# Last layer, left half: the residual add on GpSimd instead of VectorE, its stores issued by ScalarE

## The chip, the cores and the metric

One core of a Trainium2 chip runs the whole program in one launch. The metric is device microseconds. Before the change three runs took 2939.29 us in the median (2937.05 to 2940.01). The engines are called as in the profile: PE is TensorE (PEld its weight loads), DVE is VectorE, ACT is ScalarE, POOL is GpSimd, SP is SyncE. Each engine works through its own instructions strictly in the order in which they were written; engines wait for one another by semaphores.

## The reference

Two layers work on 1024 latent tokens and 256 context tokens of 1024 channels: first a convolution module, then grouped-query attention, each followed by a SwiGLU. The last layer (i = 1) is, cut to what the change touches:

```
yx, yc = attention_module(hx, hc, ...)                       # ends in @ wo
x  = x + g_x * rmsnorm(yx, norm_g[1, 1])                     # residual: the add that is moved
fx = rmsnorm(x, norm_g[1, 2]) * (1.0 + scf_x) + shf_x        # input of the FFN
x  = x + gf_x * rmsnorm((silu(fx @ w1) * (fx @ w3)) @ w2, norm_g[1, 3])
```

All of it is float32. Layer 1 no longer carries the context tokens.

## The kernel before, in words

Activations lie transposed: channels on the 128 partitions in 8 tiles (k = 0 to 7, `KT`), tokens along the free dimension. The latent tokens go in two halves of 512, left and right. To get float32 exactness from TensorE each operand is split in a high and a low part (`hi`, `lo`), and each product is three matmuls: hi·hi, hi·lo, lo·hi (L172 to L174 in `mm3`, L183 to L185 in `mm3s`). ACT writes the high part, DVE the low one.

In the last layer attention runs as a stream of units (scores L1116, softmax L1122 and L1124, transposes L1134, their split into `T2` by ACT at L1137 and DVE at L1138, and the products with V at L1140 and L1141). The left half's attention comes first. While it ends, the right half's attention is put in as background work: `pump` takes a few steps of it after each step of the foreground. So the left half's output projection, its two norms and its FFN are written into the same instruction streams as the right half's attention.

Between the left half's output projection and its FFN stands `post_pre2` (L738). PE sums squares into columns (L746). DVE works out two reciprocal roots by Newton steps on 128x4 numbers (L343 to L351): `r1` for the norm of the attention output, `r2` for the norm of the new x. PE spreads each over the partitions (L735). For each k the loop then does

- L761: y = y * column * p1, on DVE, with p1 a copy of the first spread in SBUF (`sm`);
- L763: y = y + xr, the residual add (xr is the tile `HS` in the left half);
- L764: the store of y to `x3d` in HBM, read again for the last residual some 600 us later;
- `apply`: t = y * column * p2 on DVE (L399, p2 still in PSUM), hi = t + shift on ACT (L404, into `T6`), lo = t + shift - hi on DVE (L405, into `T3`).

The FFN's first step (ft = 0) multiplies w1 and w3 with these hi and lo, k by k: six matmuls of 128x512 for each k at L183 to L185, 48 in all, called the first sweep here. Its next step begins at L172, with w1 of ft = 1.

`post_pre2` is called twice: for the left half (L1521, `keep` False) straight through, without background steps between, and for the right half (L1529, `keep` True) as background work. A scheduler in the framework below orders what each engine issues by priority, so the written order of a loop isn't kept; the orders below are those of the built programs.

Of the kernel before, what the change touches and what calls it, by code (L numbers as in the profile page):

```python
# [12 lines left out]
ALU = mybir.AluOpType  # L13
# [42 lines left out]
class Kern:  # L56
# [681 lines left out]
    def post_pre2(self, ybox, xv, ps, xdst, ftags, box, keep=False):  # L738

        nc = self.nc  # L740
        (y, yacc), more, xr = ybox
        accs = (yacc, *more)
        for i, acc in enumerate(accs):
            for j in range(4):
                with self.later():
                    nc.tensor.matmul(ps[:, 4 * i + j:4 * i + j + 1], lhsT=acc[:, j * P:(j + 1) * P],  # L746
                                     rhs=self.c["ones"], start=True, stop=True)
        ys = [ps[:, 4 * i:4 * i + 4] for i in range(3)]
        v = self.tiny([P, 16], "nv")[:, :4]
        nc.vector.tensor_scalar(out=v, in0=ys[0], scalar1=1.0 / D, scalar2=EPS, op0=ALU.mult, op1=ALU.add)  # L750
        r1 = self.rsqrt(v, 4)
        p1 = self.sm(512)
        nc.scalar.copy(p1, self.spread(r1, self.bank("st")))
        r2 = self.rsqrt(self.add_sq(ys, r1, xv), 4)
        p2 = self.spread(r2, self.bank("st"))
        yield self.pace
        hi, lo = self.halves(*ftags, 512)
        box.append((hi, lo))
        for k in range(KT):
            yk = y[:, k, :]  # L760
            nc.vector.scalar_tensor_tensor(out=yk, in0=yk, scalar=self.col[1][0][1][:, k:k + 1], in1=p1,  # L761
                                           op0=ALU.mult, op1=ALU.mult)
            nc.vector.tensor_tensor(yk, yk, xr[:, k, :], op=ALU.add)  # L763
            nc.gpsimd.dma_start(xdst[:, k], yk)  # L764
            self.apply(yk, p2, 1, 2, ((0, 512, 0),), hi, lo, k, xr[:, k, :] if keep else None)
            yield 2 * self.pace

# [956 lines left out]
```

## Time and profile before

| what | value |
|---|---|
| median of three runs | 2939.29 us |
| profiled execution, its own time | 2938.98 us |
| its span, first to last instruction | 2937.2 us |
| around the span | 1.8 us |
| PE, DVE, ACT, POOL busy | 97%, 74%, 45%, 8% |
| mean granted TensorE clock | 0.987 of full speed |

A busy share is an average over stages that have different limits: PE is busy for nearly the whole span, so what counts is where it stands still. Times in the rows are from the start of the span, and a record may overlap the next one of its engine: where instructions follow each other without a wait, the time between two starts is what one costs.

### The profile page before, as it was taken

The numbers are of one execution on the slowest core, as the hardware profiler recorded it, in microseconds if no ns is written. First come the engines' busy times: TensorE is split into PE (matmuls) and PEld (weight loads), VectorE is DVE, ScalarE is ACT, GpSimd is POOL, SyncE is SP. The second block draws the span as 40 slices with busy tenths as digits, with TensorE's granted clock in tenths as the row PEclk, the third lists the DMA queues.
The fourth block names the chain that finished last, engine by engine and source line by source line (L and its number), as shares of the span: only waits on it lengthen the run. The fifth ranks groups of instructions, "written<-read, shape, count | busy, mean of one in ns | idle before, by whom it ended". The sixth has DMA issues, their size and how long they took to land.

```text
span 2937.2 us, 42731 instructions
## 1 busy us (share of the span) xinstructions
PE 2847.7 (97%) x16462; PEld 2446.1 (83%) x16462; DVE 2160.7 (74%) x3746; ACT 1335.5 (45%) x2229; POOL 222.6 (8%) x377
## 2 busy tenths in 40 slices
PE   7999989999999999999999999989999999999998
PEld 6888877888888889989888787767777778889997
DVE  6887788847556378877786899786666666786777
ACT  5222255532222245544445688645555543444444
POOL 0000001011022001000011111110000000010000
PEclk9999999999999999999999999999999999999999
DMA  6443444334356224333345211322222143353332
GB/s 249 140 120 98 116 131 145 135 116 143 115 175 198 65 74 165 114 104 112 109 156 170 88 46 46 97 87 81 66 73 83 60 149 99 110 170 104 102 98 75
DMA packets 131755, 336.58 MB, mean 115 GB/s; under 512 B 31328, under 2 KB 52864, under 8 KB 130656
## 3 DMA queue, kind: packets, MB, share of 16 engines
q1 hardware_dynamic: 78016, 222.33, 24.1%
q0 software_dynamic: 29344, 103.83, 10.7%
q10 hardware_dynamic: 24192, 7.70, 1.1%
q8 instruction: 129, 2.11, 0.3%
q14 instruction: 74, 0.61, 0.1%
HBM read 289.50 MB, written 38.93 MB: 112 GB/s over the span
## 4 chain that ended last, share of the span: by engine, by line
PE 86%; DVE 7%; ACT 2%; issue 2%; DMA 2%; ACTq 0%; POOL 0%; SPq 0%; DVEq 0%; POOLq 0%
PE ps L172 15%; PE ps L173 15%; PE ps L174 15%; PE ps L875 4%; PE ps L877 4%; PE ps L876 4%; PE ps L1116 4%; PE ps L1134 4%; PE ps L1140 2%; PE ps L454 2%; PE ps L455 2%; PE ps L456 2%; PE ps L1141 2%; PE ps L185 1%; PE ps L183 1%
## 5 line engine op out<-in xcount | busy, mean ns | idle before, releaser
L172 PE MATMUL ps<-T,wh 128*128 128x512 f32 (+1 forms) x1360 | 502.5, 370 | 1.4 <-ACT T L161 0.8
L174 PE MATMUL ps<-T,wl 128*128 128x512 f32 (+1 forms) x1360 | 500.4, 368 | 2.0 <-DVE wl L148 2.0
L173 PE MATMUL ps<-T,wh 128*128 128x512 f32 (+1 forms) x1312 | 481.4, 367 | 0.2 <-DVE T L164 0.2
L144 ACT CAST wh<-wr 128x1024 fp32r<-128x1024 f32 (+1 forms) x217 | 225.0, 1037 | 419.9 <-PE ps L173 307.2
L148 DVE TENSOR_TENSOR wl<-wr,wh 128x1024 fp32r<-128x1024 f32 (+1 forms) x217 | 261.9, 1207 | 168.5 <-ACT wh L144 167.1
L875 PE MATMUL ps<-T,wh 128*128 128x256 f32 x1092 | 310.7, 285 | 5.0 <-ACT wh L161 4.5
L876 PE MATMUL ps<-T,wh 128*128 128x256 f32 x1092 | 306.5, 281 | 0.0
L877 PE MATMUL ps<-T,wl 128*128 128x256 f32 x1092 | 305.4, 281 | 0.2 <-DVE wl L164 0.2
L1138 DVE TENSOR_TENSOR T<-ps,T 128x512 fp32r<-128x512 f32 x320 | 216.8, 687 | 107.6 <-ACT T L1137 106.8
L172 PEld LDWEIGHTS ps<-T,wh 128*128 128x128 f32 x1360 | 257.8, 190 | 43.7 <-ACT T L1506 1.7
L174 PEld LDWEIGHTS ps<-T,wl 128*128 128x128 f32 x1360 | 257.7, 190 | 42.4 <-DVE wl L148 2.2
L173 PEld LDWEIGHTS ps<-T,wh 128*128 128x128 f32 x1312 | 248.5, 189 | 38.2 <-DVE T L164 1.3
L1137 ACT CAST T<-ps 128x512 fp32r<-128x512 f32 x320 | 186.0, 586 | 191.1 <-PE ps L1134 177.6
L173 PE MATMUL ps<-HS,wh 128*128 128x512 f32 x656 | 257.9, 393 | 0.0
L172 PE MATMUL ps<-HS,wh 128*128 128x512 f32 x608 | 238.4, 392 | 0.9 <-ACT wh L144 0.9
L174 PE MATMUL ps<-HS,wl 128*128 128x512 f32 x608 | 237.5, 391 | 0.0
L875 PEld LDWEIGHTS ps<-T,wh 128*128 128x128 f32 x1092 | 206.1, 189 | 11.2 <-ACT wh L161 6.7
L876 PEld LDWEIGHTS ps<-T,wh 128*128 128x128 f32 x1092 | 206.6, 189 | 0.5
L877 PEld LDWEIGHTS ps<-T,wl 128*128 128x128 f32 x1092 | 206.2, 189 | 0.6 <-DVE wl L164 0.4
L1134 PE MATMUL ps<-cst,T 128*128 128x128 f32 x1100 | 189.6, 275 | 3.2 <-DVE T L1138 3.1
L1122 DVE TENSOR_SCALAR_CACHE_REDUCE T<-ps,rq 128x1280 f32<-128x1280 f32 x110 | 170.0, 1546 | 27.9 <-PE ps L1116 22.1
L1134 PEld LDWEIGHTS ps<-cst,T 128*128 128x128 f32 x1100 | 132.6, 141 | 49.5 <-DVE T L1138 30.8
(377 smaller groups left out, 6195.9 us busy)
## 6 DMA issues: line engine op xcount, KB each, us to landing
wr<-in_w SPq DMA_DIRECT2D x170, 512.0 KB, 3.6
wr<-in_pw SPq DMA_DIRECT2D x35, 512.0 KB, 3.5
HV<-in_wmodT POOLq DMA_DIRECT2D x56, 256.0 KB, 4.1
q<-in_wmodT POOLq DMA_DIRECT2D x56, 256.0 KB, 3.9
KB<-in_w SPq DMA_DIRECT2D x24, 512.0 KB, 3.6
HR<-in_w SPq DMA_DIRECT2D x23, 512.0 KB, 3.7
q<-in_w SPq DMA_DIRECT2D x23, 512.0 KB, 4.2
q<-qsd POOLq DMA_DIRECT2D x32, 256.0 KB, 3.3
```

What stands on the lines that cost most here:

```text
L144: nc.scalar.copy(hi, raw)
L148: nc.vector.tensor_tensor(lo, raw, hi.bitcast(F32), op=ALU.subtract)
L172: nc.tensor.matmul(out[:, :n], lhsT=wh, rhs=xh, start=k == 0, stop=False)
L173: nc.tensor.matmul(out[:, :n], lhsT=wh, rhs=xl, start=False, stop=False)
L174: nc.tensor.matmul(out[:, :n], lhsT=wl, rhs=xh, start=False, stop=k == nk - 1)
L875: nc.tensor.matmul(out, lhsT=wh, rhs=bh, start=first and k == 0, stop=False, **skip)
L876: nc.tensor.matmul(out, lhsT=wh, rhs=bl, start=False, stop=False, **skip)
L877: nc.tensor.matmul(out, lhsT=wl, rhs=bh, start=False, stop=k == 3, **skip)
L1122: nc.vector.tensor_scalar(out=pt, in0=sc, scalar1=rq[:, h:h + 1], scalar2=None, op0=ALU.mult, op1=ALU.min, accum_out=mn)
L1134: nc.tensor.transpose(tp[:, h * P:(h + 1) * P], Ps[h][:, j * P:(j + 1) * P], c["ident"])
L1137: nc.scalar.copy(ph, tp)
L1138: nc.vector.tensor_tensor(pl, tp, ph.bitcast(F32), op=ALU.subtract)
```

## The change

In the left half the add L763 goes from DVE to POOL, and the eight stores L764 from POOL's queue to ACT's. The right half (`keep` True) stays as it was.

```
             nc.vector.scalar_tensor_tensor(out=yk, in0=yk, scalar=self.col[1][0][1][:, k:k + 1], in1=p1,
                                            op0=ALU.mult, op1=ALU.mult)
-            nc.vector.tensor_tensor(yk, yk, xr[:, k, :], op=ALU.add)
-            nc.gpsimd.dma_start(xdst[:, k], yk)
+            (nc.vector if keep else nc.gpsimd).tensor_tensor(yk, yk, xr[:, k, :], op=ALU.add)
+            (nc.gpsimd if keep else nc.scalar).dma_start(xdst[:, k], yk)
             self.apply(yk, p2, 1, 2, ((0, 512, 0),), hi, lo, k, xr[:, k, :] if keep else None)
```

The scheduler answers with another order on four engines; SP's is unchanged. In the pieces below `T_16045` is y, `HS` is xr, `sm` is p1, `sb` is t, `T_16582` and `T_16583` are hi and lo; `T_13569` and `T_14068` are softmax rows of the right half's attention and `T_13571` their transposed split; `nr`, `nq` and `nh` are the 128x4 numbers of the Newton steps.

First place: POOL ahead of the FFN, the difference (lines with + are the change's).

```order
 L1147 COPY sb<-sums 128x256
 L1450 DMA od<-sb 128x2x128
-L764 DMA x3d<-T_16045 128x512 x8
+L763 ISA
+L763 TENSOR_TENSOR T_16045<-T_16045,HS 128x512 x8
 L1147 COPY sb<-sums 128x256
 L1102 DMA q<-qsd 128x4x128
```

The eight stores are gone from POOL; in their place stand the eight adds, and ahead of them one instruction without operands that the builder puts in (it has the engine load the code that the adds need, and waits for nothing).

The same place on DVE, the end of its piece of the difference: the last steps of the loop's first part and of the Newton steps for r2.

```order
-L763 TENSOR_TENSOR T_16045<-T_16045,HS 128x512 x2
+L351 SCALAR_TENSOR_TENSOR nr<-nq,nr 128x4
+L761 SCALAR_TENSOR_TENSOR T_16045<-T_16045,col_7910,sm 128x512
+L349 TENSOR_TENSOR nq<-nr 128x4
+L761 SCALAR_TENSOR_TENSOR T_16045<-T_16045,col_7910,sm 128x512
+L350 TENSOR_TENSOR nq<-nq,nh 128x4
+L1138 TENSOR_TENSOR T_13571<-ps,T_13571 128x512
+L351 SCALAR_TENSOR_TENSOR nr<-nq,nr 128x4
 L399 SCALAR_TENSOR_TENSOR sb<-T_16045,col_7912,ps 128x512 x3
```

DVE now runs all eight L761 in a row, each followed by one small Newton step, then one L1138 of the attention and the last Newton step; before, six L761 and six L763 stood there, and two of each followed further down.

Second place: ACT from the copy of p1 to the FFN's first weights, the whole difference.

```order
 L753 COPY sm<-ps 128x512
 L1137 CAST T_13571<-ps 128x512
+L764 DMA x3d<-T_16045 128x512 x8
+L1137 CAST T_13571<-ps 128x512
 L404 ACTIVATE T_16582<-sb,mod_103 128x512 x8
-L1137 CAST T_13571<-ps 128x512
 L144 CAST wh<-wr_73 128x1024
 L838 ACTIVATE sm<-ps 128x512
```

All eight stores, and a cast of the attention, now stand ahead of the first L404.

Third place: PE between the end of the left half's norms and the first sweep, one piece of the difference.

```order
 L1140 MATMUL ps<-T_13571,HR 128x512
+L1134 MATMUL ps<-cst,T_13569 128x128
 L735 MATMUL ps<-cst,nr 128x128 x4
+L1134 MATMUL ps<-cst,T_14068 128x128
+L1134 MATMUL ps<-cst,T_13569 128x128
+L1134 MATMUL ps<-cst,T_14068 128x128
+L1141 MATMUL ps<-T_13571,HR 128x512
+L1140 MATMUL ps<-T_13571,HR 128x512
 L183 MATMUL ps<-T_16582,wh 128x512 x2
```

Four transposes, one L1141 and one L1140 of the attention have moved ahead of the sweep; by L172 of ft = 1 both programs have issued the same matmuls, and from there on the orders are equal but for waits.

## Rows read from the trace of the kernel before

**Rows 1.** The page: the chain that ended last, shares by engine.

```profile
PE 86%; DVE 7%; ACT 2%; issue 2%; DMA 2%; ACTq 0%; POOL 0%; SPq 0%; DVEq 0%; POOLq 0%
```

**Rows 2.** Chain in order of time, 1941 to 1952: start, length, engine, line.

```profile
1941.33 0.75 DVE T L761
...
1948.45 1.20 DVE T L763 x2
1949.66 0.67 DVE sb L399
1950.35 0.73 ACT T L404
1951.12 1.22 PE ps L183 x2
```

**Rows 3.** Windows: stretch, length, busy of five engines, granted clock, DMA share, GB/s.

```profile
1945.00:1950.00 5.00, 1.11 (x4) 0.71 (x4) 5.00 (x12) 0.00 (x0) 1.68 (x5) 0.50 0.53 202
1950.00:1955.00 5.00, 3.87 (x9) 2.62 (x10) 5.00 (x9) 2.72 (x5) 0.49 (x1) 0.53 0.27 105
1955.00:1960.00 5.00, 5.00 (x23) 4.05 (x22) 5.00 (x8) 1.36 (x3) 0.20 (x1) 1.00 0.00 0
```

**Rows 4.** Timeline of DVE: start, length, line, operation, idle before.

```profile
1941.33 0.75 DVE L761 SCALAR_TENSOR_TENSOR T<-T,col,sm 128x512 f32<-128x512 f32 x1
...
1942.07 0.75 DVE L761 SCALAR_TENSOR_TENSOR T<-T,col,sm 128x512 f32<-128x512 f32 x1
```

**Rows 5.** Line L763: durations in ns (min, median, max), first and last start.

```profile
L763 DVE TENSOR_TENSOR T<-T,HS x8: 683/684/684, 1942.8 to 1959.4; 128x512 f32<-128x512 f32 x8
```

**Rows 6.** Timeline of POOL, 1895 to 1945.

```profile
1921.87 0.71 POOL L1450 DMA_DIRECT2D od<-sb  x1 [6.04 <-DVE sb L1156]
1943.79 1.22 POOL L764 DMA_DIRECT2D x3d<-T  x2 [21.21 <-DVE nr L351]
```

**Rows 7.** POOL's work on SBUF: its copies L1147, its small fills.

```profile
L1147 POOL COPY sb<-sums x32: 394/402/1365, 1605.4 to 2363.0; 128x256 f32<-128x256 f32 x32
...
L1271 POOL MEMSET KB<- 128x16 f32 x3 | 0.2, 113 | 48.8 <-PE ps L242 48.8
```

**Rows 8.** Timelines of DVE and POOL at the longest of these copies.

```profile
2133.81 1.22 DVE L148 TENSOR_TENSOR wl<-wr,wh 128x1024 fp32r<-128x1024 f32 x1
2134.95 0.68 DVE L1138 TENSOR_TENSOR T<-ps,T 128x512 fp32r<-128x512 f32 x1
...
2133.91 1.36 POOL L1147 COPY sb<-sums 128x256 f32<-128x256 f32 x1
```

**Rows 9.** Issues of DMAs from ACT's queue: durations in ns.

```profile
L472 ACTq DMA_DIRECT2D KB<-HR x64: 552/622/1559, 63.5 to 346.9; - x64
...
L1604 ACTq DMA_DIRECT2D outT<-T x1: 385/385/385, 2932.8 to 2932.8; - x1
```

**Rows 10.** Timeline of ACT, 1940 to 1967.

```profile
1950.35 2.04 ACT L404 ACTIVATE T<-sb,mod 128x512 fp32r<-128x512 f32 x3 [8.57 <-DVE sb L399]
...
1965.88 0.58 ACT L1137 CAST T<-ps 128x512 fp32r<-128x512 f32 x1
1966.35 1.06 ACT L144 CAST wh<-wr 128x1024 fp32r<-128x1024 f32 x1
```

**Rows 11.** Timeline of PE, 1941 to 1968.

```profile
1947.85 1.11 PE L735 MATMUL ps<-cst,nr 128*128 128x128 f32 x4 [5.51 <-DVE nr L351]
...
1962.16 0.60 PE L1134 MATMUL ps<-cst,T 128*128 128x128 f32 x4
1962.51 0.48 PE L1141 MATMUL ps<-T,HR 128*128 128x512 f32 x1
1962.83 0.41 PE L184 MATMUL ps<-T,wh 128*128 128x512 f32 x1
...
1967.40 0.50 PE L172 MATMUL ps<-T,wh 128*128 128x512 f32 x1 [0.39 <-DVE sm L839]
```

**Rows 12.** The page: DMA issues, with KB and median us to landing.

```profile
HV<-in_wmodT POOLq DMA_DIRECT2D x56, 256.0 KB, 4.1
```

## The prediction

> **What bounds the kernel now.** I read first the chain that ended last, by engine: 86% of it is PE and 7% DVE [rows 1]. So most stages are limited by matmuls, and work taken off DVE pays only where PE waits for DVE. The chain in order of time shows such a place at the change: from 1941.33 to 1950.35 us it runs over L761, L763 and L399 on DVE, then over one L404 on ACT, and at 1951.12 the first sweep starts on PE [rows 2]. The windows say the same in shares: from 1945 to 1950 DVE is busy 5.00 of 5.00 us, ACT 0.00 and PE 1.11, with a granted clock of 0.50, the lower of TensorE's two levels (1.2 GHz); it is 0.53 in the next 5 us and 1.00 from 1955 on, so PE pays for its rest a little beyond it [rows 3]. Here the add stands on the path that sets the end. From L172 at 1967.40 [rows 11] both orders are the same and PE goes on nearly without a gap, so I take the shift of that L172 as the change of the whole time.
>
> **What leaves DVE.** Ahead of the first L399 stood six L763. Each record is 684 ns [rows 5]; in the chain two of them take 1.20 us [rows 2], so 0.60 us each and 3.6 us in all. In their place come the two L761 that stood further down and one L1138 of the attention. Two L761 start 0.74 us apart with a small Newton step between them [rows 4], so all eight take 8 x 0.74 = 5.9 us, from 1941.33 to 1947.25; L1138 adds about 0.6 (its record is 0.68 [rows 8]), and the last Newton step ends at about 1948.0. Before, the spread L735 that waits for that step started at 1947.85 [rows 11]. So the reciprocal root is no earlier than it was: the order has eaten the gain. Undisturbed, L399 would start at about 1949.2 in place of 1949.6, a gain of 0.4 us and no more.
>
> **What POOL does in its place.** No add of two arrays on POOL is in this trace, so I bound it. Its copies of 128x256 take 402 ns in the median, its small fills 113 ns [rows 7]: about 0.1 us to start, and 0.30 for 256 elements. For 512 elements, with the second input read beside the first for nothing, that makes 0.1 + 0.6 = 0.7 us; with the two inputs read one after the other, 0.1 + 1.2 = 1.3 us. I take 1.1, above the middle, since only the upper end has a mechanism; eight adds are then 8.8 us. The Trainium skill ("GPSIMD Engine Reference", section Performance versus the Vector engine) has 4497 ns for such an add of 2048 elements; a quarter of that is 1.12, and by it the sum would be 0.2 us more. No run here shows it.
>
> **Can the adds run beside L761?** This decides the result. Of the 32 copies on POOL one took 1365 ns, against 402 in the median [rows 7]. It started at 2133.91, just after L148 on DVE had begun at 2133.81, and it ended at 2135.27, about 0.3 us after DVE had gone on to its next instruction at 2134.95 [rows 8]. L148 reads two arrays in SBUF (`wr` and `wh`); the L1138 that followed reads one and PSUM, and the copy finished beside it. I read this as: POOL's reading of SBUF stood still until DVE's two-input instruction was through. L761 reads y and p1, both in SBUF, and the small Newton steps behind each read two as well. So the 5.9 us of DVE work and the 8.8 us of adds go one after the other, in whatever turns: the last add ends at 1941.33 + 5.9 + 8.8 + 0.1 for a first wake-up = 1956.1. The Trainium skill states it as a rule ("SBUF — State Buffer", section Who interferes with whom): a DVE instruction with two SBUF inputs and a GpSimd instruction that reads SBUF exclude each other, and the one that comes second waits for the whole of the other. By that rule, the trace agrees in the one place that can show it; without it the last add would end at 1942.2 + 8.8 = 1951.0, which is the first rival's sum.
>
> **What stands behind the adds on ACT.** ACT stood idle for 8.57 us ahead of its first L404 at 1950.35 [rows 10], so eight issues have room there. But in the new order all eight stores are ahead of L404, each waits for its add, and ACT works in order: the first L404, which needs only the first add, now waits for the last. That is the wait the change adds. Behind it stand PE's sweep (it needs hi) and DVE's L405. Issues from ACT took 385 and 622 ns [rows 9]; I take 0.5 for the last, the others hide between adds. With 0.1 for the signal ACT is free at 1956.7. Then come the moved cast L1137, 0.47 from its start to the next one's [rows 10], and L404 with 0.73 [rows 2]: the sweep starts at about 1957.95, 6.8 us later than 1951.12. The two last stores also wait for two loads of SP's, lanes of the same counters; these were issued long before and have landed: nothing. POOL's eight issues go (two in 1.22 us [rows 6]); POOL was waiting between them, so that gains nothing. The store itself is read hundreds of us later.
>
> **What is given back.** Three transposes of a group of four, one L1141 and a gap have left the sweep, and run while PE waits: from 1962.16 to 1962.51 the four, to 1962.83 the L1141 [rows 11], so 0.26 + 0.32, and 0.16 of waiting near 1961.5. That is 0.7 us. PE restarts on the lower clock before and after, so this costs the same. DVE keeps ahead: its L405 come in threes at 0.66 us each, while PE needs six matmuls for each k.
>
> **Sum.** 6.8 - 0.7 = +6.1 us, if DVE gets its eight L761 and the last Newton step through early. If the turns alternate, that step stands behind the last add, and the spread (1.11 us [rows 11]) and some transposes come after it on the path: 1.3 us more, +7.4. I take the middle, +6.7. On the profiled execution's 2938.98 (span 2937.2 and 1.8 around it) that is 2945.7 us. The median of the runs, 2939.29, is 0.3 above that execution, which I leave out. With adds at 0.7 and at 1.3 us the sum goes to 6.1 - 3.2 = +2.9 and 7.4 + 1.6 = +9.0: the forecast's own range is 2941.9 to 2948.0.
>
> **The rivals.**
>
> First, no exclusion: the adds overlap L761, and the one long copy had another cause. The last add ends at 1951.0, ACT is free at 1951.6, the sweep starts at 1952.8, 1.7 late, less 0.7: +1.0 us, 2940.0. For it: it is one copy in 32. Against it: the length fits L148 to 0.3 us, and the typical copies that I could set beside DVE's work ran beside instructions with one SBUF input.
>
> Second, on the other side: no exclusion and quick adds. Below 0.98 us each, unhindered, the last store no longer holds L404 beyond what the transposes give back, and the change gains. At 0.7 the gate is L399 again: sweep at 1950.7, 0.4 early, and 0.7 given back: -1.1 us, 2937.9. It needs both the absent exclusion and the lower bound.
>
> Third, the instruction ahead of the adds. POOL has nothing to do from 1922.6 to the first add at 1942.1, 19.5 us [rows 6], so I cost it at nothing. If the code comes in only with the first add, POOL starts late. This trace has no such load; with about 4 us, as a DMA of 256 KB takes to land [rows 12], it would be +4 on top, 2949.7. The Trainium skill ("GPSIMD Engine Reference", section Architecture, Instruction dispatch) has about 6 us for the first call to freshly loaded code, which would make 2951.7; no run here shows it.
>
> **How the numbers follow.** Forecast 0.80, first rival 0.10, second 0.04, third 0.06. A measurement of this kernel can tell about 0.2%, 5.9 us, from no change. The forecast's sums lie on both sides of that bound, from +2.9 to +9.0 with the middle at +6.7; I give two thirds of it to slower, 0.54, and 0.26 to same. With the third rival slower is 0.60. Both first rivals are within the bound: same is 0.26 + 0.10 + 0.02 = 0.38, and 0.02 is left for faster. The range has to reach the first rival below (2940.0) and just past the forecast's upper end: 2940.0 to 2948.5.
>
> **What would show it.** In the changed profile: eight L763 on POOL, with about 14 us from the first L761 to the end of the last add; records or start distances on POOL or of L761 on DVE well above 1.1 and 0.74 us while both run, which would be the exclusion; the first L404 right behind the last store on ACT; PE's first L183 near 1958, and L172 of ft = 1 near 1974. If the adds start 0.74 us apart from 1942.2 and L761 keeps its pace, the exclusion is wrong. If the first L183 starts before L764's last issue, the wait on ACT is wrong. If L172 is late and the end isn't, the claim is wrong that PE carries the shift to the end.

## The result, and the profile after

| | median us | runs (lowest to highest) | ratio to before, 95% interval |
|---|---|---|---|
| before, all runs | 2940.90 | 15 (2937.05 to 2944.93) | |
| the change | 2945.76 | 15 (2940.74 to 2948.58) | 1.0017 [1.0010, 1.0024] |

The 15 runs of the kernel before take in the three that were known ahead; their median is 1.6 us higher than that of the three (2939.29). The change is slower by 4.9 us; the interval makes that 2.9 to 7.1 us. Its profiled execution has a span of 2944.6 us against 2937.2, 7.4 us more.

The windows of the changed kernel, with the columns of [rows 3], show PE standing still for nearly ten microseconds, 1945 to 1955, in which DVE and POOL are both busy:

```profile
1945.00:1950.00 5.00, 0.00 (x0) 0.00 (x0) 5.00 (x8) 0.00 (x0) 4.15 (x3) 0.50 0.40 157
1950.00:1955.00 5.00, 0.09 (x1) 0.09 (x1) 5.00 (x7) 0.00 (x0) 4.37 (x4) 0.50 0.27 105
1955.00:1960.00 5.00, 4.60 (x13) 3.03 (x14) 3.74 (x6) 2.43 (x4) 0.46 (x1) 0.50 0.27 105
1960.00:1965.00 5.00, 5.00 (x19) 3.94 (x19) 5.00 (x9) 2.04 (x3) 0.74 (x1) 0.82 0.00 0
```

PE (first column after the length) did 1.11 and 3.87 us of work in the first two stretches before; now 0.00 and 0.09. Both engines look busy, but a record that lasts long isn't work: the timelines of the two show it. First DVE (start, length, line, operation):

```profile
1940.76 0.75 DVE L761 SCALAR_TENSOR_TENSOR T<-T,col,sm 128x512 f32<-128x512 f32 x1
1941.43 0.16 DVE L349 TENSOR_TENSOR nq<-nr 128x4 f32<-128x4 f32 x1
1941.51 0.75 DVE L761 SCALAR_TENSOR_TENSOR T<-T,col,sm 128x512 f32<-128x512 f32 x1
1942.17 1.22 DVE L350 TENSOR_TENSOR nq<-nq,nh 128x4 f32<-128x4 f32 x1
1943.31 1.83 DVE L761 SCALAR_TENSOR_TENSOR T<-T,col,sm 128x512 f32<-128x512 f32 x1
1945.07 0.15 DVE L351 SCALAR_TENSOR_TENSOR nr<-nq,nr 128x4 f32<-128x4 f32 x1
1945.14 0.74 DVE L761 SCALAR_TENSOR_TENSOR T<-T,col,sm 128x512 f32<-128x512 f32 x1
...
1954.18 0.68 DVE L1138 TENSOR_TENSOR T<-ps,T 128x512 fp32r<-128x512 f32 x1
1954.78 0.70 DVE L351 SCALAR_TENSOR_TENSOR nr<-nq,nr 128x4 f32<-128x4 f32 x1
```

Then POOL, with the idle time before it in brackets:

```profile
1941.60 2.99 POOL L763 TENSOR_TENSOR T<-T,HS 128x512 f32<-128x512 f32 x2 [21.16 <-DVE nq L349]
1945.22 3.00 POOL L763 TENSOR_TENSOR T<-T,HS 128x512 f32<-128x512 f32 x2 [0.63 <-DVE nr L351]
1948.84 3.00 POOL L763 TENSOR_TENSOR T<-T,HS 128x512 f32<-128x512 f32 x2 [0.63 <-DVE nq L350]
1952.46 2.99 POOL L763 TENSOR_TENSOR T<-T,HS 128x512 f32<-128x512 f32 x2 [0.63 <-DVE nq L349]
```

A Newton step on 128x4 numbers, L350, that takes 0.16 us elsewhere took 1.22, and the L761 behind it 1.83 in place of 0.75; then the next pair of short records. There are four such turns, the last with L1138 and the final L351 in the place of an L761. One turn of two L761 and two adds lasts 1945.22 - 1941.60 = 3.62 us. Two L761 at a pace of 0.66 and two adds at 1.14 (from the start of the held L350 to the next start, 1943.31 less 1942.17) make 3.60. Since the 1.14 is read from the same turn, an add that nothing hinders is the better test: it takes 1.25 us (p1_in_psum below), and with it the sum is 3.82. So no more than 0.2 us of a turn overlaps. From the first L761 to the end of the last add it is 1955.45 - 1940.76 = 14.7 us; about 14 were named as the sign, and the forecast's sum had 14.8. L1138, with one input in PSUM, ran at 0.68 beside the last adds.

On ACT, which is to be set beside [rows 10]:

```profile
1943.40 12.41 ACTq L764 DMA_DIRECT2D x3d<-T  x8
...
1957.33 0.59 ACT L1137 CAST T<-ps 128x512 fp32r<-128x512 f32 x1 [16.11 <-DMA x3d<-T]
1957.81 1.95 ACT L404 ACTIVATE T<-sb,mod 128x512 fp32r<-128x512 f32 x3
```

On PE, beside [rows 11]:

```profile
1954.91 0.47 PE L1134 MATMUL ps<-cst,T 128*128 128x128 f32 x1 [13.15 <-DVE T L1138]
1955.54 1.11 PE L735 MATMUL ps<-cst,nr 128*128 128x128 f32 x4
1956.45 0.84 PE L1134 MATMUL ps<-cst,T 128*128 128x128 f32 x3
...
1958.59 1.22 PE L183 MATMUL ps<-T,wh 128*128 128x512 f32 x2
...
1973.71 0.50 PE L172 MATMUL ps<-T,wh 128*128 128x512 f32 x1 [0.38 <-DVE sm L839]
```

The sweep starts 17.83 us behind the first L761; before it was 1951.12 - 1941.33 = 9.79. The sweep itself, to L172, is shorter, 15.12 against 16.28 us. L172 comes 32.95 us behind the first L761 in place of 26.07: 6.9 us late.

Two views disagree on what held L1137. The chain of waits names a store:

```profile
1952.47 3.00 POOL T L763 x2
1955.47 0.02 issue
1955.49 1.85 DMA x3d<-T
1957.34 0.59 ACT T L1137
```

The timeline of ACT puts the issue of the last store at 1955.49, done 0.33 us later, and on PE the transposes L1134 that feed the cast L1137 end at 1957.29. Only one of the two can have held it; the second experiment decides.

### The profile page after: what moved, and what is told of

Its sections match the earlier page's. It is cut to its first block, busy times and chain, and to the rows that moved or that the text cites. A ratio compares the mean times of both kernels' runs of the same rounds, so it can differ in the third digit from the quotient of the medians.

```text
span 2944.6 us, 42728 instructions
## 1 busy us (share of the span) xinstructions
PE 2851.4 (97%) x16462; PEld 2448.3 (83%) x16462; DVE 2164.6 (74%) x3738; ACT 1334.4 (45%) x2229; POOL 229.4 (8%) x377
## 4 chain that ended last, share of the span: by engine, by line
PE 87%; DVE 7%; ACT 2%; issue 2%; DMA 2%; POOL 0%; ACTq 0%; SPq 0%; DVEq 0%; POOLq 0%
PE ps L172 15%; PE ps L173 15%; PE ps L174 15%; PE ps L875 4%; PE ps L877 4%; PE ps L876 4%; PE ps L1116 4%; PE ps L1134 4%; PE ps L1140 2%; PE ps L454 2%; PE ps L455 2%; PE ps L456 2%; PE ps L1141 2%; PE ps L185 1%; PE ps L183 1%
## 5 line engine op out<-in xcount | busy, mean ns | idle before, releaser
L172 PE MATMUL ps<-T,wh 128*128 128x512 f32 (+1 forms) x1360 | 503.3, 370 | 0.7 <-DVE sm L839 0.4
L1138 DVE TENSOR_TENSOR T<-ps,T 128x512 fp32r<-128x512 f32 x320 | 216.8, 687 | 108.6 <-ACT T L1137 107.8
L172 PEld LDWEIGHTS ps<-T,wh 128*128 128x128 f32 x1360 | 258.1, 190 | 43.2 <-ACT T L1506 1.7
L1137 ACT CAST T<-ps 128x512 fp32r<-128x512 f32 x320 | 185.9, 586 | 208.0 <-PE ps L1134 178.3
L172 PE MATMUL ps<-HS,wh 128*128 128x512 f32 x608 | 238.5, 392 | 0.9 <-ACT wh L144 0.9
L1134 PE MATMUL ps<-cst,T 128*128 128x128 f32 x1100 | 190.9, 276 | 16.3 <-DVE T L1138 16.3
L1134 PEld LDWEIGHTS ps<-cst,T 128*128 128x128 f32 x1100 | 133.6, 142 | 62.7 <-DVE T L1138 43.6
```

Source lines behind the costliest of these rows:

```text
L172: nc.tensor.matmul(out[:, :n], lhsT=wh, rhs=xh, start=k == 0, stop=False)
L1134: nc.tensor.transpose(tp[:, h * P:(h + 1) * P], Ps[h][:, j * P:(j + 1) * P], c["ident"])
L1137: nc.scalar.copy(ph, tp)
L1138: nc.vector.tensor_tensor(pl, tp, ph.bitcast(F32), op=ALU.subtract)
```

## The experiments

The theory (A): an add on POOL and a DVE instruction with two inputs in SBUF exclude each other; the whole loss is their serial sum and the order that follows. The rivals: the adds are simply slow on POOL; the stores hold ACT; the order of the Newton steps is the loss. A stage serves as measure, from L750 (start of the Newton steps) to the first L172 of ft = 1: 33.10 us before, 40.72 after. In it, PE's busy time is given with the granted clock, since PE's time is longer where the clock is lower. The windows that span it, one kernel each (columns as in [rows 3]), are these.

Before:

```profile
1934.30:1967.40 33.10, 23.49 (x92) 16.49 (x92) 30.36 (x71) 12.71 (x19) 4.78 (x9) 0.80 0.17 64
```

After:

```profile
1932.99:1973.71 40.72, 24.92 (x92) 17.95 (x92) 33.64 (x63) 12.51 (x19) 12.73 (x9) 0.73 0.13 52
```

PE's idle time in the stage is 33.10 - 23.49 = 9.6 us before and 15.8 after, 6.2 more; the other 1.4 us of the difference are PE working longer, at a mean clock of 0.73 against 0.80.

Each ratio below is taken to runs of the kernel before made beside that experiment (median 2940.2 us for the first four, 2938.66 for the last two; the change had 2940.90), so medians that were not taken beside each other aren't subtracted. Each trace is one execution.

### The first spread left in PSUM (p1_in_psum)

L761 then reads one array in SBUF and one in PSUM; adds and stores as in the change.

```
-        p1 = self.sm(512)
-        nc.scalar.copy(p1, self.spread(r1, self.bank("st")))
+        p1 = self.spread(r1, self.bank("st"))
+        if keep:
+            p1s, p1 = p1, self.sm(512)
+            nc.scalar.copy(p1, p1s)
```

> The changed kernel, with one thing altered: in the left half p1 is no longer copied to SBUF, the scaling reads it where PE put it, in PSUM (line numbers behind it grow by two: scaling L763, add L765, store L766). Measured by the stretch from L750 to the start of L172 of ft = 1: 33.1 us in the kernel before, 40.7 in the change. Theory A: a DVE instruction that reads two arrays in SBUF and an add on POOL shut each other out. Then the eight scalings, which now read one array in SBUF, keep 0.66 to 0.75 us each although adds run beside them; only the small Newton steps still wait for adds; the last add ends about 10.5 us after the first scaling's start instead of 14.7; the stretch is 37.4 us (36.5 to 38.5), and the time about 3 us under the change's, 1.0005 to 1.001 of before. Theory B: any DVE work beside POOL's adds is stretched, or the adds are slow by themselves. Then scalings again take up to 1.8 us, and the stretch stays at 40 to 41.

Measured: 1.0004 [0.9995, 1.0014] of before, 2941.02 us; the stage is 37.63. Timeline of DVE (L763 is here the scaling, L765 the add):

```profile
1943.34 0.73 DVE L763 SCALAR_TENSOR_TENSOR T<-T,col,ps 128x512 f32<-128x512 f32 x1
1944.00 0.64 DVE L349 TENSOR_TENSOR nq<-nr 128x4 f32<-128x4 f32 x1
1944.56 0.73 DVE L763 SCALAR_TENSOR_TENSOR T<-T,col,ps 128x512 f32<-128x512 f32 x1
...
1951.17 0.16 DVE L351 SCALAR_TENSOR_TENSOR nr<-nq,nr 128x4 f32<-128x4 f32 x1
```

POOL:

```profile
1940.91 9.81 POOL L765 TENSOR_TENSOR T<-T,HS 128x512 f32<-128x512 f32 x8 [19.83 <-DVE nv L728]
```

No scaling is stretched any more (0.73 where 1.83 stood) and the eight adds run back to back, 9.81 / 8 = 1.23 us each (1.25 a record), while scalings run beside them. The same operands, one of them read from another memory: the exclusion hangs on the second SBUF input. The stage is 3.1 us shorter than the change's; theory A had 37.4 for it. The first scaling starts 0.6 us of that sooner (7.17 us behind L750 in place of 7.77), since it needs no copy. In the whole the ratio falls by 0.0013, about 4 us (1.0004 against 1.0017); stores_on_sp below, which is as slow as the change and was measured beside this run, lies 4.8 us higher in the median (2945.8 against 2941.02). The small steps still read two arrays in SBUF and last 0.64 us for 0.16: each waits until the add that runs is through, so DVE's row of steps goes at POOL's pace, and the last step for r2 still comes behind the last add. It ends 18.42 us behind L750, against 13.49 before; that is the 4.5 us of stage that are left, and a little more. The rule that the prediction named ("SBUF — State Buffer", section Who interferes with whom, of the Trainium skill) exempts DVE instructions with at most one SBUF input, outside what it calls DVE's two-port modes; the scalings of this run agree, at 0.73 us.

### The stores issued by SP (stores_on_sp)

```
-            (nc.gpsimd if keep else nc.scalar).dma_start(xdst[:, k], yk)
+            (nc.gpsimd if keep else nc.sync).dma_start(xdst[:, k], yk)
```

> The changed kernel, with the left half's eight stores issued by SP instead of ACT; the adds stay on POOL. Theory A (from the trace of the change): the stores on ACT hold nothing, since the last is issued at 1955.8 and the first L404 waits for the last Newton step, which the adds hold up, for the spread behind it and for the cast L1137. Then the stretch from L750 to L172 of ft = 1 stays at 40.7 us within 0.5, and the time within 0.1% of the change. Rival (the step in the recorded prediction): the first L404 waits for the last store. Then it starts at least 1 us sooner and the stretch is at most 39.7.

Measured: 1.0018 [1.0009, 1.0027], 2945.8 us. Timeline of ACT:

```profile
1958.29 0.59 ACT L1137 CAST T<-ps 128x512 fp32r<-128x512 f32 x1 [16.11 <-PE ps L1134]
1958.77 1.95 ACT L404 ACTIVATE T<-sb,mod 128x512 fp32r<-128x512 f32 x3
```

L404 comes 1958.77 - 1933.95 = 24.82 us behind L750; in the change it was 1957.81 - 1932.99 = 24.82. With no store on ACT nothing moved, and the idle time of 16.11 us is now put down to PE's L1134. So the chain's "DMA x3d<-T" was the wrong one of two events, and the stores hold nothing. The stage is 39.69, 1.0 shorter and outside the 0.5 that theory A allowed. All of it lies behind L404: this execution's clock rose sooner within the sweep (0.99 in the window 1960 to 1965, against 0.82 in the change's). The rival had the right total for another reason: its earlier L404 did not come. It also shows that the clock alone can move this stage by 1 us from one execution to the next.

### The stores alone (stores_alone)

The kernel before, with its adds on DVE, and only the stores on ACT.

```
-            (nc.vector if keep else nc.gpsimd).tensor_tensor(yk, yk, xr[:, k, :], op=ALU.add)
+            nc.vector.tensor_tensor(yk, yk, xr[:, k, :], op=ALU.add)
```

(an edit of the changed kernel.)

> The kernel before, with the left half's eight stores issued by ACT instead of POOL; the adds stay on DVE. Theory A: the stores by themselves cost nothing: stretch from L750 to L172 of ft = 1 33.1 us within 0.5, ratio to before 1.000 within 0.0007. Rival: their issues (0.4 to 0.6 us each, ahead of and between the L404) delay the high parts by 1 to 4 us; stretch 34 or more.

Measured: 0.9992 [0.9983, 1.0001], 2939.27 us. ACT:

```profile
1943.99 6.50 ACTq L764 DMA_DIRECT2D x3d<-T  x6
1950.82 2.04 ACT L404 ACTIVATE T<-sb,mod 128x512 fp32r<-128x512 f32 x3 [8.57 <-DVE sb L399]
```

L404 waits 8.57 us for L399 as before [rows 10], and comes 9.02 us behind the first L761 (1941.80), as before (1950.35 - 1941.33). The stage is 34.28: over theory A's upper end of 33.6 and within the rival's 34 or more, but not by the rival's cause, which is a late L404. Of the 1.2 us beyond the kernel before, 0.7 lie ahead of the first L761, where nothing edited has run yet: it comes 7.77 us behind L750 here, 7.77 in the change too, and 7.03 before, with PE's granted clock between the two at 0.63 here, 0.68 in the change and 0.76 before. The other 0.4 lie in the sweep (16.71 us to L172 against 16.28), where PE came to its fast pace 5.2 us behind the start in place of 3.8. So 0.7 of the 7.6 us by which the change's stage is longer belongs to the clock of that execution, and the distance from the first L761, 6.9, is the cleaner measure. This half of the change costs nothing in the time that the interval can tell. The loss lies with the adds.

### One SBUF input everywhere, Newton steps first (one_sbuf_operand)

p1 and t are in PSUM, and the scaling's column is tied to r2 (0 * r2 + column), so that no two-input step stands beside the adds; SP issues the stores. The edit of p1 is that of p1_in_psum and isn't repeated. L768 is here the scaling, L770 the add.

```
-        t = self.sb(n)
+        t = self.bank("tt")[:, :n] if "tt" in self.banks else self.sb(n)
...
+        g = self.col[1][0][1]
+        if not keep:
+            g = self.tiny([P, KT], "gt")
+            nc.vector.scalar_tensor_tensor(out=g, in0=r2[:, 0:1].to_broadcast([P, KT]), scalar=0.0,
+                                           in1=self.col[1][0][1], op0=ALU.mult, op1=ALU.add)
...
-        self.set_banks(mm=[0], st=[1, 6], pt=[5], av=[7])
+        self.set_banks(mm=[0], st=[1, 6], pt=[5], av=[7], tt=[3, 4])
```

> A version built on theory A: adds on POOL, but every large DVE instruction of the left half's loop reads at most one array in SBUF: p1 stays in PSUM, and t is written to two free PSUM banks instead of SBUF. The scaling's column is made to depend on r2, so that the Newton steps run first and in a row; stores by SP. (New lines: column L761, scaling L768, add L770, store L771.) Theory A: adds follow each other about 1.1 us apart, scaling, L399 and L405 keep 0.65 to 0.8 us each beside them, DVE has 16 us to do in the loop instead of 20.6, and L172 of ft = 1 comes 31 us (29.5 to 32.5) behind L750 instead of 33.1; ratio to before about 0.9993. Theory B: DVE is stretched whatever it reads, or PSUM operands and the later start cost what the adds gave: 33 us or more.

Measured: 1.0006 [0.9997, 1.0015], 2941.5 us; the stage is 34.01, not 31, and so in theory B's range (33 or more). DVE:

```profile
1943.54 1.41 DVE L768 SCALAR_TENSOR_TENSOR T<-T,gt,ps 128x512 f32<-128x512 f32 x2
1945.68 0.75 DVE L399 SCALAR_TENSOR_TENSOR ps<-T,col,ps 128x512 f32<-128x512 f32 x1 [0.73 <-POOL T L770]
1946.91 0.76 DVE L399 SCALAR_TENSOR_TENSOR ps<-T,col,ps 128x512 f32<-128x512 f32 x1 [0.48 <-POOL T L770]
```

The adds, durations in ns (min, median, max):

```profile
L770 POOL TENSOR_TENSOR T<-T,HS x8: 1264/1272/1277, 1944.4 to 1959.2; 128x512 f32<-128x512 f32 x8
```

No record is stretched on either engine, against the first half of B (DVE stretched whatever it reads): an unhindered add is 1.27 us. The second half, that the arrangement costs what the adds gave, fits. The first scaling comes 8.78 us behind L750 (7.03 before, 7.77 in the change), DVE waits 0.48 to 0.73 us for an add four times, and POOL 1.52 for a scaling four times: the two engines now hand rows to and fro. My expectation left these waits out.

### The same with the adds on DVE (adds_back_on_dve)

```
-            (nc.vector if keep else nc.gpsimd).tensor_tensor(yk, yk, xr[:, k, :], op=ALU.add)
+            nc.vector.tensor_tensor(yk, yk, xr[:, k, :], op=ALU.add)
```

> The arrangement of the run one_sbuf_operand (first spread and the scaled rows stay in PSUM, second reciprocal root ahead of the first scaling), with the eight residual adds back on DVE. It tells whether the add on POOL pays at all once no DVE instruction of the stage shuts it out. DVE's work from the first scaling to the last lo part is 8 x (0.66 + 0.60 + 0.66 + 0.66) = 20.6 us plus two attention steps of 0.6, against 16 + 1.2 and 2.5 us of waits in one_sbuf_operand. Theory A (POOL's add pays what it takes off DVE, less the waits): first scaling 8.8 us behind L750, last L405 ends 30.7 behind it in place of 28.4, and PE, starved for each k, needs some 3.5 us more: stage (L750 to L172 of ft = 1) 34 to 35.5 us, 0 to 1.5 longer than one_sbuf_operand's 34.0. Rival (each hand-over between DVE and POOL costs more than the add saves): stage below 33.5 us. Ratio to the kernel before 1.000 to 1.001 by A, 0.9995 to 1.000 by the rival; the stage decides.

Measured: 1.0014 [1.0005, 1.0024], 2943.96 us; the stage is 36.11, 0.6 over the expected range, on A's side:

```profile
1935.06:1971.17 36.11, 29.54 (x89) 18.88 (x88) 29.85 (x70) 10.77 (x16) 0.00 (x0) 0.67 0.15 59
```

and one_sbuf_operand's:

```profile
1934.76:1968.77 34.01, 27.48 (x90) 18.49 (x89) 25.71 (x62) 10.80 (x16) 10.05 (x8) 0.74 0.16 62
```

DVE is busy 4.1 us longer, PE idle as long (6.6 us against 6.5), and PE works 2.1 us longer at a clock of 0.67 against 0.74. So POOL's add seems to pay where nothing shuts it out, 2.1 us of this stage, and the gain appears in PE's pace rather than in its idle time. This isn't shown beyond doubt: the clock alone moved the stage by 1.0 us between the change and stores_on_sp, and the two ratios, 1.0006 and 1.0014, lie the same way with intervals that overlap. Against the kernel before it buys nothing, since this arrangement without POOL is the slower one.

### The Newton steps first, alone (newton_first)

The kernel before with the tied column only (p1 in SBUF, adds on DVE, stores by POOL).

> The kernel before (adds on DVE, stores by POOL, first spread copied to SBUF), only with the second reciprocal root worked out ahead of the first scaling (the column is tied to r2 by a product with zero). It tells whether the order of the Newton steps alone explains part of the change's loss. Theory A: the order costs what the scalings no longer hide, stage 33.5 to 35.5 us against 33.1 of before, since DVE's 8 x (0.74 + 0.60 + 0.66 + 0.66) = 21.3 us now stand between the first scaling and the last lo part; no record of POOL or DVE is stretched, since no add runs on POOL. Rival (the order was the loss): stage at 31 or less, and a ratio of 0.9993 or less.

Measured: 0.9996 [0.9987, 1.0006], 2938.06 us; the stage is 35.13, within A's range:

```profile
1935.50:1970.63 35.13, 28.26 (x104) 18.47 (x103) 31.64 (x73) 12.68 (x20) 5.14 (x9) 0.82 0.16 60
```

The rival falls: with the adds on DVE, the order of the steps is neither a loss nor a gain that the ratio can tell. Not tried is the change itself, adds on POOL and p1 in SBUF, with the Newton steps first. The stage is 2 us longer and the whole isn't; the scheduler put more of the attention into it (104 records on PE against 92), which fits. So the stage compares kernels with the same work in it, as the change with the first three runs; for the last three the ratio is the safer measure, and among them only the pair with the same order but for the adds is read by its stage. No run beats the kernel before by more than its interval.

## Why the prediction came out right, and where it did not

The forecast was 2945.7 us within 2940.0 to 2948.5, and 2945.76 was measured. That the two meet to 0.1 us is luck. The forecast added 6.7 us to one execution of the kernel before, at 2938.98; the median of its 15 runs is 2940.90, so the measured change is 4.9 us (2.9 to 7.1), 1.8 below the forecast's middle. Where the 6.7 can be read directly, from the first L761 to L172, it is 6.9. The forecast gave 0.60 to a loss beyond its bound of 0.2% (5.9 us) and 0.38 to one within it: the loss is clear of zero, and within the bound. Point by point:

- **The exclusion.** This was right, and p1_in_psum shows it: the one stretched copy among 32 [rows 7, 8] had been read rightly. 5.9 + 8.8 us one after the other were forecast to end 14.8 us behind the first L761; measured 14.7.
- **The price of an add.** It was taken at 1.1 us between 0.7 and 1.3. An unhindered add measures 1.25 to 1.27, at the upper end, where the two inputs read one after the other would put it; a held step of DVE waits 1.14 of that. The sum was right since in it only this part counts; that it comes so near the 1.1 is luck, since the forecast meant the whole add. By the Trainium skill ("GPSIMD Engine Reference", section Performance versus the Vector engine) the estimate of a quarter of its 2048-element add was 1.12: this agrees with the 1.14, and is 0.13 to 0.15 short of the record.
- **Nothing saved ahead of r2.** The reciprocal root did not come earlier, as forecast, but by another way. It came at 1954.78 + 0.70 = 1955.48, held by the adds to the end, 14.7 us behind the first L761; one of the forecast's two branches had 1948.0, which is 6.7 behind it.
- **The wait added on ACT.** This step failed. The prediction had the first L404 stand behind the last store, and named that as a sign to look for. The last store was out at 1955.82, L404 began at 1957.81, and with the stores on SP it began equally late. What held it was the branch that the sum carried as "if the turns alternate": the last Newton step L351, after it the spread L735, three transposes and the cast. Its sum was 1.3 us above the other: 8.1 to the start of the sweep (6.8 + 1.3). Measured is 17.83 - 9.79 = 8.0. The branch that counts made +7.4 in all, and what was given back was under-sized by 0.5, which brings it to the 6.9. So the middle of two branches, +6.7, was right in size by luck: only one of them is real.
- **Given back.** 0.7 forecast, 1.2 measured (16.28 - 15.12). The transposes left the sweep as forecast; in the timelines PE also came to its fast pace (matmuls of at most 0.40 us) sooner behind the sweep's start, after 3.2 us against 3.8. How the other 0.5 divides isn't settled: in stores_on_sp, with the same order on PE, the sweep took 14.09 us.
- **Instruction load ahead of the adds.** Its cost of nothing was right: the first add began at 1941.60, right behind the first L761, after 21.16 us of idle time on POOL. The trace has the instruction ahead of the adds, a `MODIFY_POOL_CONFIG`, at 1920.4, so whatever it brings in had 21 us to come (no row shows a load itself). The third rival falls.
- **No exclusion, quick adds.** The first two rivals fall: an add and an L761 don't advance beside each other, and an add takes 1.25 us, above the 0.98 below which the second could have come about.
- **PE carries the shift to the end.** L172 is 6.3 us later in the two profiled spans, the end 7.4. In the medians it is 4.9, within 2.9 to 7.1: the profiled execution of the kernel before lies 1.9 us under its median, that of the change 0.6 over. One execution of each can't tell these from each other, and so this claim is neither shown nor refuted to better than 2 us.

## What to carry to other kernels

Before an elementwise step goes from DVE to POOL, list what DVE runs beside it and count the SBUF inputs of each instruction, down to the 128x4 ones: those with two waited for whole POOL instructions here, however small they were, and POOL for them. Then add the two engines' times rather than take the larger. An operand left in PSUM lifted the exclusion, but no arrangement tried came out ahead of the kernel before: POOL's rows were waited for at once. And where a wait's named releaser and the timeline disagree, move the suspected instruction to another queue before believing either.

## What was not expected of the hardware

- In p1_in_psum two small steps with a single SBUF input were held beside an add too, L343 for 0.73 us and L345 for 0.58, while L347, the same kind of instruction, took 0.16:

```profile
1941.47 0.73 DVE L343 TENSOR_SCALAR nq<-nv 128x4 int32<-128x4 int32 x1
1942.11 0.16 DVE L347 TENSOR_SCALAR nh<-nv 128x4 f32<-128x4 f32 x1
...
1942.84 0.58 DVE L345 TENSOR_SCALAR nr<-nq 128x4 int32<-128x4 int32 x1
```

Why the int32 ones are held, whether by one of the two-port modes that the exemption above leaves out, and whether L347 just met a free moment, wasn't tried.

- While both engines had work ready they went in turns, in each of the change's four rounds: an add, a small step, an add, an L761. A 128x4 step (0.16 us) thus waited as long (1.14 us) as an L761 did (1.83 - 0.75 = 1.1). Such turns aren't the rule. In stores_alone a copy on POOL, 0.40 us in the median [rows 7], took 3.29: DVE ran the last L405, two L761 and two L763 through beside it, all with two inputs in SBUF, and the copy ended at 1960.85, 0.34 us after L399, with one, had begun. It is a second sign of the exclusion, with POOL as the loser:

```profile
1957.56 3.29 POOL L1147 COPY sb<-sums 128x256 f32<-128x256 f32 x1 [35.69 <-DVE T L405]
```

Beside it on DVE:

```profile
1957.98 1.40 DVE L761 SCALAR_TENSOR_TENSOR T<-T,col,sm 128x512 f32<-128x512 f32 x2
1959.30 1.28 DVE L763 TENSOR_TENSOR T<-T,HS 128x512 f32<-128x512 f32 x2
1960.51 1.39 DVE L399 SCALAR_TENSOR_TENSOR sb<-T,col,ps 128x512 f32<-128x512 f32 x2
```

- Part of the idle time that PE saved came back as slower work: from the change to p1_in_psum PE's idle time in the stage falls from 15.8 to 11.1 us and its busy time grows from 24.9 to 26.5. Its sweep began 4.3 us sooner behind L750, but PE came to its fast pace 5.6 us behind that start in place of 3.2. The mean clock of the stage is 0.73 in both.
